# A list-scheduled hybrid decoder layer: inputs regrouped on the queues, weights in 4 KB runs, matmul costs taken from measured durations

## The chip, the cores and the metric

One Trainium2 chip, one core. The metric is the device time of one launch in microseconds (us). The kernel before takes 172.94 us (median of 3 runs, 172.69 to 173.69). PE is TensorE, DVE VectorE, ACT ScalarE, POOL GpSimd, SP SyncE, which issues most of the transfers.

## What is computed

One layer, T = 256 tokens, D = 1024, all in float32. The norm's reciprocal root is applied behind the projection, its gains ahead of it.

```
h = rmsnorm(x, pre_norm_g)
proj = einsum('btd,dc->btc', h, w_in)                 # 1024 x 4104
p_gdn, p_hgrn, p_moba, p_diff = split(proj)
y = concat([gdn_branch(p_gdn), hgrn2_branch(p_hgrn),
            moba_branch(p_moba), diff_branch(p_diff)])
x = x + rmsnorm(einsum('btc,cd->btd', y, w_out), post_norm_g)
```

Each branch has 4 heads of 64. The gated delta net (gdn) runs a short convolution over q, k and v, a gate g and, per chunk of 64 tokens, a triangular inverse; HGRN2 is a gated linear recurrence in chunks of 16; MoBA and the differential attention are causal softmax attentions with a distance penalty.

## The kernel before, in words

**The work.** The transposed x (1024 x 256, eight slices k of 128 rows) is scaled by the gains and split into a rounded high part `hT_hi` (ACT) and a remainder `hT_lo` (DVE). The weights come in pieces of two slices k and one of eight column blocks (512 columns, 520 for `gv`): 32 pieces of 512 KB, into six buffers `raw`. Each piece is split as well, `whi` on ACT and `wlo` on DVE (`split`, from line 423), into four buffers each, and each product is three matmuls, hi x hi, lo x hi and hi x lo, into `pj`. So no piece can reach PE before its transfer, one ACT instruction and one DVE instruction, and no buffer comes free before PE has used it. The first piece comes as two transfers (slices k = 0 and k = 1). `xs` is x once more, untransposed, for the norm and the residual sum.

**The first transfers** (lines 400 to 412, `piece` from 427). Five parts of the transposed x: the slice k = 0 on ACT's queue, the other four (k = 1; 2 and 3; 4 and 5; 6 and 7) on SP's queue between the weights. `pc` holds 35 columns of constants, the gains among them, and comes second on ACT's queue. A burst of bf16 matmuls on zeros (`wA<-g_nb`) runs on PE meanwhile.

**The order.** Every operation is recorded with a cost (`mm` 219, `act` 234, `vec` 240, `dma` 267) and `plan` (287) simulates the engines: of what is ready on an engine, the operation of the highest rank goes first. Rank is the longest path of costs to the end, plus a boost, plus `LEAD` of its part of the program (g is the delta net, h HGRN2, m and M MoBA, d and D the differential attention, o the output projection). `emit` (372) issues in that order, so nearly all instructions carry line 381 and table loads line 379. Three rules bend the order. Once PE has run an operation on part of its columns, others of that sort that are ready go ahead of full ones. An ACT function whose table set is not loaded waits while something else of a rank within `HOLD` is ready. A full matmul of 256 columns is charged 108.7 ns, a DVE subtraction of 1024 elements 1131 ns:

```
full = 1.667 if rhs.dtype == F else .417
... max(n * full, m * full, 53 if rhs.dtype == F else 107) + 2      # mm, PE
base = 66 if eng == "DVE" else 90                                   # vec
cost = base + (rate if eng == "DVE" else 2.2) * n + 61 * ...
```

On the chip nothing is simulated: each engine runs its list in order and waits on semaphores.

**Names.** `g_u`, `g_au`, `g_g`: the steps to the gate g, through ACT's exponential and logarithm. `g_ee`, `g_d`, `g_nb`, `g_y`, `g_ya`, `g_xa`: the triangular inverse on DVE, fifteen steps of one shuffle and two products; `g_xa` goes back to PE. `kf`, `lf`: keys and queries of the attentions; `wB<-kf,lf` their scores.

Of the kernel before, what the change touches and what calls it, by code (L numbers as in the profile page):

```python
# [21 lines left out]
F = mybir.dt.float32  # L22
# [3 lines left out]
AF = mybir.ActivationFunctionType  # L26
OP = mybir.AluOpType
# [62 lines left out]
class Op:  # L90
    __slots__ = ("eng", "fn", "args", "kw", "cost", "need", "preds", "succs", "rank", "left", "at", "order", "boost", "groups", "work", "part", "lat")


class Core:
# [72 lines left out]
    def record(self, eng, fn, cost, writes, reads, args, kw, need=None):  # L167
        op = Op()
        op.eng, op.fn, op.args, op.kw, op.cost, op.need = eng, fn, args, kw, cost, need
        op.preds, op.succs, op.boost, op.groups, op.work = set(), [], self.boost, (0, 1, 2, 3), 0.0  # L170
        op.part, op.lat = self.part, self.LAT[eng]
        me = len(self.ops)
        for w, aps in ((False, reads), (True, writes)):
            for ap in aps:
                name = ap.tensor.name
                if name in self.psum:

                    b = self.psum[name]
# [40 lines left out]
    def mm(self, out, lhsT, rhs, start=True, stop=True, **kw):  # L219
        n, m = self.size(rhs), lhsT.shape[1]  # L220
        full = 1.667 if rhs.dtype == F else .417
        self.record("PE", "matmul", max(n * full, m * full, 53 if rhs.dtype == F else 107) + 2, [out], [lhsT, rhs], (out,),
                    dict(lhsT=lhsT, rhs=rhs, start=start, stop=stop, **kw))
        p, m = self.rows(out)
        o = self.ops[-1]
        if 2 < m < 128:
            o.groups = tuple(range(p // 32, (p + m + 31) // 32))
        o.work = n * full * self.rows(rhs)[1] / 128

# [57 lines left out]
    def plan(self, noise=None):  # L287
# [21 lines left out]
        order, cur = [], 6  # L309
        cols, small, work = [0.0] * 4, False, {}  # L310
        while events:
# [5 lines left out]
            for e, q in ready.items():  # L317
# [76 lines left out]

def _build(c, x, xt, w_in, w_out, cst, pcol, prow, out, dbg):
    mm, tr, act = c.mm, c.tr, c.act
# [25 lines left out]

    BLOCKS = {"gkq": [(C_GQ, 512)], "gv": [(C_GV, 520)], "hqf": [(C_HQ, 512)], "hiz": [(C_HI, 512)],
              "mqk": [(C_MQ, 512)], "dqk": [(C_DQ, 512)], "mvz": [(C_MV, 512)], "dvz": [(C_DV, 512)]}
    RAW, HI, LO = {}, {}, {}

    def piece(key, k):

        if (key, k) not in HI:
            t = c.tmp("raw", [128, 2, 520], bufs=6)  # L430
            first = not HI
            (c0, w), = BLOCKS[key]
            part = w_in[k * 128:(k + 2) * 128, c0:c0 + w].rearrange("(k p) n -> p k n", p=128)
            lead = sum(1 for q in HI if q[0] != "o")
# [758 lines left out]
def _arrays(inputs):  # L1193
# [8 lines left out]
                                                      "diff_lq2", "diff_lk2", "post_norm_g")])[None]  # L1202
    return {"x": a["x"].reshape(T, D),
            "xt": np.ascontiguousarray(a["x"].reshape(T, 8, 128).transpose(2, 1, 0)).reshape(128, 8 * T),
            "w_in": a["w_in"][0], "w_out": a["w_out"][0], "cst": _shape_constants(),
            "pcol": np.ascontiguousarray(pcol), "prow": np.ascontiguousarray(prow)}

# [16 lines left out]
```

## Time and profile before

| | |
|---|---|
| median of 3 runs (lowest, highest) | 172.94 us (172.69, 173.69) |
| the profiled execution | 172.76 us |
| its span (first to last instruction) | 171.1 us |
| instructions | 3627 |
| transfers | 27.24 MB, 159 GB/s in the mean |
| ACT table loads | 17, 1283 ns each |
| `wlo` subtractions on DVE | 41, 1196 ns in the mean |

The profile is of one execution, so sums are made against its 172.76 us; 1.7 us of that lie outside the span. In the rows further below a line reads: start or busy time, engine, program line, operation, out<-in, shape, and in square brackets the idle time of the engine ahead of it with what ended that.

### The profile page before, as it was taken

Reading aid. Unit: us, or ns where it says so; the run is one execution under the profiler, and the core shown is the slowest. Engines: PE = TensorE matmul, PEld = TensorE weight load, DVE = VectorE, ACT = ScalarE, POOL = GpSimd, SP = SyncE. Lnnn points to the kernel's source line nnn. Section 1 sums busy time; section 2 is a strip of 40 time slices with the busy share of each in tenths; the row PEclk is TensorE's granted clock in tenths of the full one; section 3 lists DMA queues with packets and bytes.
Section 4 is the critical chain, followed back from the end, with each engine's and each line's share of the span. In section 5 each row is a group of like instructions: output and inputs, shape, how many; then the busy total and the mean of one; then the engine's idle time right before and its main releaser. Section 6 shows DMA issues by size and latency. Waiting matters only on the chain.

```text
span 171.1 us, 3627 instructions
## 1 busy us (share of the span) xinstructions
PE 161.9 (95%) x1358; PEld 141.9 (83%) x1358; DVE 132.2 (77%) x353; ACT 116.7 (68%) x219; POOL 15.7 (9%) x35
## 2 busy tenths in 40 slices
PE   7599999999999999999999999999999999999960
PEld 5399999999798999999799777776788878998850
DVE  0568559898988899999977968978798847559472
ACT  3375566799979864541299999989879925445440
POOL 8000000000000700000604106000000000000000
PEclk9999999999999999999999999999999999999998
DMA  4779997878872448619921998332702400000033
GB/s 137 259 269 322 368 352 264 336 254 236 181 266 87 91 130 206 159 15 256 265 52 40 216 339 254 81 128 63 245 0 98 151 0 0 4 0 0 0 123 123
DMA packets 14832, 27.24 MB, mean 159 GB/s; under 512 B 1504, under 2 KB 2784, under 8 KB 14816
## 3 DMA queue, kind: packets, MB, share of 16 engines
q1 hardware_dynamic: 13376, 25.30, 46.9%
q0 software_dynamic: 1152, 1.57, 4.2%
q8 instruction: 10, 0.16, 0.4%
q10 hardware_dynamic: 288, 0.15, 0.3%
q14 instruction: 6, 0.05, 0.1%
HBM read 24.14 MB, written 1.05 MB: 147 GB/s over the span
## 4 chain that ended last, share of the span: by engine, by line
PE 83%; DMA 8%; ACT 4%; DVE 1%; issue 1%; DVEq 0%; ACTq 0%
PE pj L381 58%; PE gB L381 8%; PE gA L381 7%; PE wB L381 6%; DMA raw<-in_w_in_dram 5%; PE wA L381 4%; DMA pc<-in_pcol_dram 3%; ACT whi L381 1%; ACT L379 1%; ACT qk4k L381 1%; DVE b4k L381 1%; DVE wlo L381 1%; ACT b4k L381 0%; DVEq L1220 0%; ACT hT_hi L381 0%
## 5 line engine op out<-in xcount | busy, mean ns | idle before, releaser
L381 DVE TENSOR_TENSOR wlo<-raw,whi 128x1024 fp32r<-128x1024 f32 (+2 forms) x41 | 48.0, 1196 | 10.5 <-ACT whi L381 7.8
L381 ACT ACTIVATE whi<-raw 128x1024 fp32r<-128x1024 f32 (+2 forms) x40 | 41.1, 1045 | 19.6 <-PE pj L381 9.5
L381 PE MATMUL pj<-hT_hi,whi 128*128 128x256 f32 x144 | 37.5, 293 | 2.1 <-ACT hT_hi L381 2.1
L381 PE MATMUL pj<-hT_lo,whi 128*128 128x256 f32 x144 | 37.3, 292 | 0.0
L381 PE MATMUL pj<-hT_hi,wlo 128*128 128x256 f32 x144 | 31.7, 292 | 0.0
L381 PEld LDWEIGHTS pj<-hT_hi,whi 128*128 128x128 f32 x144 | 27.4, 198 | 2.9 <-ACT hT_hi L381 2.6
L381 PEld LDWEIGHTS pj<-hT_lo,whi 128*128 128x128 f32 x144 | 27.1, 196 | 0.9 <-issue 0.7
L381 PE MATMUL pj<-whi,hT_lo 128*128 128x512 f32 (+2 forms) x80 | 26.6, 350 | 0.0
L381 PEld LDWEIGHTS pj<-hT_hi,wlo 128*128 128x128 f32 x144 | 23.6, 195 | 0.6 <-issue 0.3
L379 ACT ACT_TABLE_LOAD x17 | 21.8, 1283 | 2.0 <-PEq L1214 1.7
L381 PE MATMUL pj<-whi,hT_hi 128*128 128x512 f32 (+2 forms) x64 | 21.4, 350 | 0.0
L381 PE MATMUL pj<-wlo,hT_hi 128*128 128x512 f32 (+2 forms) x64 | 19.6, 347 | 0.0
L381 PEld LDWEIGHTS pj<-whi,hT_lo 128*128 128x128 f32 x80 | 15.0, 188 | 1.7
L381 PEld LDWEIGHTS pj<-whi,hT_hi 128*128 128x128 f32 x64 | 11.9, 188 | 1.4 <-issue 0.2
L381 PEld LDWEIGHTS pj<-wlo,hT_hi 128*128 128x128 f32 x64 | 10.9, 188 | 1.1
L381 ACT ACTIVATE prob<-prob,mx 128x128 f32<-128x128 f32 (+1 forms) x24 | 10.6, 445 | 0.5 <-DVE mx L381 0.5
L381 POOL DMA_DIRECT2D d_st<-d_ks x12 | 6.0, 509 | 51.2 <-ACT d_ks L381 51.2
L381 PE MATMUL pj<-whi,d_st 128*128 128x512 f32 (+1 forms) x32 | 9.6, 378 | 0.0
L381 POOL DMA_DIRECT2D d_st<-qk4k x12 | 5.9, 496 | 38.3 <-ACT qk4k L381 22.4
L381 DVE CUSTOM_DVE_ANT_0 prob<-wB,cs 128x128 f32<-128x128 f32 (+1 forms) x24 | 8.1, 351 | 1.7 <-PE wB L381 1.1
L381 PEld LDWEIGHTS pj<-whi,d_st 128*128 128x128 f32 x32 | 5.6, 188 | 1.1
L381 ACT ACTIVATE hT_hi<-prob,pc 128x256 fp32r<-128x256 f32 x8 | 3.7, 500 | 3.5 <-DMA pc<-in_pcol_dram 3.3
(266 smaller groups left out, 290.1 us busy)
## 6 DMA issues: line engine op xcount, KB each, us to landing
raw<-in_w_in_dram SPq DMA_DIRECT2D x27, 512.0 KB, 7.9
raw<-in_w_out_dram SPq DMA_DIRECT2D x8, 512.0 KB, 5.2
raw<-in_w_in_dram SPq DMA_DIRECT2D x4, 520.0 KB, 12.4
xs<-in_x_dram SPq DMA_DIRECT2D x2, 512.0 KB, 11.9
prob<-in_xt_dram SPq DMA_DIRECT2D x3, 256.0 KB, 7.7
d_st<-d_ks POOLq DMA_DIRECT2D x12, 64.0 KB, 2.1
d_st<-qk4k POOLq DMA_DIRECT2D x12, 64.0 KB, 4.3
raw<-in_w_in_dram SPq DMA_DIRECT2D x2, 256.0 KB, 4.1
```

The costliest lines, as they stand in the source:

```text
L379: nc.scalar.add_instruction(mybir.InstLoadActFuncSet(name=nc.get_next_instruction_name(), act_func_set_id=cur, ins=[], outs=[]))
L381: getattr(self.engines[o.eng], o.fn)(*o.args, **o.kw)
```

## The change

1. **Inputs.** The columns of constants and the transposed x are one array `pxt`. Its first 291 columns, the constants and the slice k = 0, come in one transfer into `px` (in the order `h_kd`, whose buffer it shares), and the four other parts of x follow it on ACT's queue. SP's queue starts with weights alone. The gains are read from `px`; `pc` is a copy made on DVE.
2. **Weights.** On the host, w_in is laid out piece by piece, so that a partition of a piece is one run of 4 KB in memory (4160 B for `gv`). In the buffer the two slices still stand 520 columns apart; only a piece of `gv` is one run there too.
3. **Scheduler.** A full matmul is charged `max(n * .446, 107) + 4.5` ns (256 columns: 118.7), each operation has a tile shape (`mode`), a change of shape is charged 95 ns and operations of the present shape are preferred; `HOLD` and `LEAD` get new values. The costs of DVE, ACT and the transfers stay.

```diff
-    HOLD = 1000
-    LEAD = {'h': -65, 'g': 9004, 'o': -15813, 'M': 4592, 'x': 3396, 'm': 1525, 'd': -18, 'D': 1459}
+    HOLD = 71859
+    SWITCH, KEEP, STAY = 95, 1e9, 10357
+    LEAD = {'h': 9467, 'g': 7491, 'o': -78342, 'M': -634, 'x': 25587, 'm': 2702, 'd': 2886, 'D': 6239}
...
-        self.record("PE", "matmul", max(n * full, m * full, 53 if rhs.dtype == F else 107) + 2, [out], [lhsT, rhs], (out,),
+        cost = max(n * full, m * full) + 2 if rhs.dtype == F else max(n * .446, 107) + 4.5
+        self.record("PE", "matmul", cost, [out], [lhsT, rhs], (out,),
...
+        k = self.rows(rhs)[1]
+        o.mode = (32 if k <= 32 else 64 if k <= 64 else 128 if k > 96 else 96, 32 if m <= 32 else 64 if m <= 64 else 128)
+        o.work = n * full * k / 128
...
-                if e == "PE" and small and len(o.groups) == 4:
-
-                    more = [x for x in q if len(ops[x[1]].groups) < 4]
+                if e == "PE" and mode != o.mode:
+
+                    more = [x for x in q if ops[x[1]].mode == mode and -x[0] > o.rank - (self.KEEP if mode != (128, 128) else self.STAY)]
...
-                    was, small = small, len(o.groups) < 4
-                    o.at = max([t] + [cols[g] + 53 * was * (1 if small else .5) for g in o.groups])
+                    if o.mode != mode:
+                        o.at = max(t, max(cols) + self.SWITCH)
+                        mode = o.mode
+                    else:
+                        o.at = max([t] + [cols[g] for g in o.groups])
...
-    XPARTS = [(0, 1), (1, 2), (2, 4), (4, 6), (6, 8)]
...
+    c.boost = turn(0)
+    c.dma(px[:, 0:P_END + T], pxt[:, 0:P_END + T], "ACT")
+    XPARTS = [(1, 2), (2, 4), (4, 6), (6, 8)]
...
-        c.dma(xr[a // 2][:, a % 2:a % 2 + b - a], xt[:, a * T:b * T].rearrange("p (k t) -> p k t", t=T), "ACT" if a == 0 else "SP")
-    c.boost = turn(0) - 0.1 * BOOST
-    c.dma(pc, pcol, "ACT")
+        c.dma(xr[a // 2][:, a % 2:a % 2 + b - a],
+              pxt[:, P_END + a * T:P_END + b * T].rearrange("p (k t) -> p k t", t=T), "ACT")
...
-            part = w_in[k * 128:(k + 2) * 128, c0:c0 + w].rearrange("(k p) n -> p k n", p=128)
+            w, o = BLOCKS[key], BLOCK_AT[key] + k * 128 * BLOCKS[key]
+            part = bass.AP(tensor=w_in.tensor, offset=w_in.offset + o, ap=[[2 * w, 128], [w, 2], [1, w]])
```

**How the order moves.** Buffer numbers are shifted by one between the two programs (`whi_93` before is `whi_94` in the change), and line 381 becomes 392.

ACT at the start of the program, first before, then in the change (`prob_67` to `prob_71` and `h_kd` hold x):

```order
L381 DMA prob_67<-in_xt_dram 128x256
L381 DMA pc<-in_pcol_dram 128x35
L379 ACT_TABLE_LOAD
L381 ACTIVATE hT_hi<-prob_67,pc 128x256
L381 ACTIVATE whi_93<-raw_92 128x512
L381 ACTIVATE hT_hi<-prob_67,pc 128x256
L381 ACTIVATE whi_96<-raw_95 128x2x512
L381 ACTIVATE hT_hi<-prob_68,pc 128x256 x2
L381 ACTIVATE whi_99<-raw_98 128x2x512
```

```order
L392 DMA h_kd<-in_pxt_dram 128x291
L392 DMA prob_68<-in_pxt_dram 128x256
L392 DMA prob_69<-in_pxt_dram 128x512
L392 DMA prob_70<-in_pxt_dram 128x512
L392 DMA prob_71<-in_pxt_dram 128x512
L390 ACT_TABLE_LOAD
L392 ACTIVATE hT_hi<-h_kd 128x256
L392 ACTIVATE hT_hi<-prob_68,h_kd 128x256
L392 ACTIVATE whi_94<-raw_93 128x512
L392 ACTIVATE hT_hi<-prob_69,h_kd 128x256 x2
L392 ACTIVATE hT_hi<-prob_70,h_kd 128x256
L392 ACTIVATE whi_97<-raw_96 128x2x512
```

The table load now stands behind five transfers, the scaling of slice k = 4 (`hT_hi<-prob_70`) stands ahead of the `whi` of slices 2 and 3, and the scaling of both halves of `prob_69` comes ahead of it too.

PE where the attention scores `wB<-kf,lf` (64 rows) stand among the projection's matmuls, before and in the change:

```order
L381 MATMUL pj_106<-hT_hi,whi_102 128x256
L381 MATMUL wB_147<-kf,lf 128x128
L381 MATMUL pj_106<-hT_lo,whi_102 128x256
L381 MATMUL pj_106<-hT_hi,wlo_103 128x256
L381 MATMUL pj_106<-hT_hi,whi_102 128x256
L381 MATMUL pj_106<-hT_lo,whi_102 128x256
L381 MATMUL pj_106<-hT_hi,wlo_103 128x256
L381 MATMUL wB_147<-kf,lf 128x128
L381 MATMUL pj_106<-hT_hi,whi_102 128x256
L381 MATMUL pj_106<-hT_lo,whi_102 128x256
```

```order
L392 MATMUL pj_91<-whi_103,hT_lo 128x256
L392 MATMUL pj_92<-hT_hi,whi_103 128x256
L392 MATMUL pj_92<-hT_lo,whi_103 128x256
L392 MATMUL wA_78<-ident,prob_68 128x128
L392 MATMUL gA_83<-g_xa,g_ee 64x64 x16
L392 MATMUL wB_148<-kf,lf 128x128 x2
L392 MATMUL wA_78<-ident,prob_68 128x128
L392 MATMUL pj_92<-hT_hi,whi_103 128x256
L392 MATMUL pj_92<-hT_lo,whi_103 128x256
L392 MATMUL pj_91<-wlo_95,hT_hi 128x256
```

The score matmuls, each alone before, now go in pairs, later, and some of them right behind another small shape. Counted over both programs, PE leaves the full shape 29 times before and 23 times in the change. The matmul `gA<-g_xa` stands 67 matmuls earlier than before.

DVE at the start of the triangular inverse, before and in the change:

```order
L381 SCALAR_TENSOR_TENSOR g_d_128<-g_ee,cs,g_d_128 128x128
L381 TENSOR_TENSOR g_kdec<-gA_82,g_kd 64x2x128
L381 SCALAR_TENSOR_TENSOR g_d_128<-g_ee,cs,g_d_128 128x128
L381 TENSOR_TENSOR wlo_100<-raw_92,whi_99 128x2x512
L381 STREAM_SHUFFLE g_nb_76<-g_d_128 128x128
L381 TENSOR_TENSOR wlo_103<-raw_95,whi_102 128x2x512
L381 TENSOR_TENSOR g_nb_76<-g_nb_76,g_y_129 128x8x15
L381 STREAM_SHUFFLE g_nb_130<-g_d_128 128x128
L381 TENSOR_TENSOR g_y_129<-g_y_129,g_nb_76 128x8x15
L381 STREAM_SHUFFLE g_nb_131<-g_d_128 128x128
L381 TENSOR_TENSOR g_nb_130<-g_nb_130,g_y_129 128x8x14
```

```order
L392 SCALAR_TENSOR_TENSOR g_d_129<-g_ee,cs,g_d_129 128x128
L392 TENSOR_TENSOR g_kdec<-gA_83,g_kd 64x2x128
L392 STREAM_SHUFFLE g_nb_77<-g_d_129 128x128
L392 STREAM_SHUFFLE g_nb_131<-g_d_129 128x128
L392 TENSOR_TENSOR g_nb_77<-g_nb_77,g_y_130 128x8x15
L392 STREAM_SHUFFLE g_nb_132<-g_d_129 128x128
L392 TENSOR_TENSOR wlo_95<-raw_108,whi_94 128x2x512
L392 TENSOR_TENSOR g_y_130<-g_y_130,g_nb_77 128x8x15
L392 TENSOR_TENSOR g_vb<-gB_115,g_beta 64x2x128
L392 TENSOR_TENSOR wlo_98<-raw_109,whi_97 128x2x512
L392 TENSOR_TENSOR g_nb_131<-g_nb_131,g_y_130 128x8x14
L392 TENSOR_TENSOR wlo_101<-raw_93,whi_100 128x2x512
```

Four `wlo` of 1024 elements now stand within the first steps of the inverse; before, seven stand within all of it. On ACT the list of the change has 9 table loads, that of before 17.

## Rows read from the trace of the kernel before

**Rows 1.** The page, parts 1 and 4: busy time by engine, and the chain by engine.

```profile
PE 161.9 (95%) x1358; PEld 141.9 (83%) x1358; DVE 132.2 (77%) x353; ACT 116.7 (68%) x219; POOL 15.7 (9%) x35
...
PE 83%; DMA 8%; ACT 4%; DVE 1%; issue 1%; DVEq 0%; ACTq 0%
```

**Rows 2.** The chain of waits, in order of time: start us, us, what.

```profile
1.23 4.96 DMA pc<-in_pcol_dram
6.85 15.73 PE pj L381 x108
...
72.62 9.35 PE pj L381 x79
81.97 1.06 PE wB L381 x4
```

**Rows 3.** Busy time of the engines from 60 to 88 us, x instructions: PE, PEld, DVE, ACT, POOL.

```profile
60.00:88.00 28.00, 28.00 (x232) 26.53 (x233) 27.17 (x107) 13.48 (x22) 2.92 (x6) 1.00 0.66 165
```

**Rows 4.** Timeline of PE: start us, us, engine line op out<-in xcount.

```profile
51.55 0.28 PE L381 MATMUL pj<-hT_hi,whi 128*128 128x256 f32 x1
51.76 0.48 PE L381 MATMUL wB<-kf,lf 64*128 64x128 f32 x2
52.18 0.38 PE L381 MATMUL pj<-hT_lo,whi 128*128 128x256 f32 x1
52.40 0.28 PE L381 MATMUL pj<-hT_hi,wlo 128*128 128x256 f32 x1
```

**Rows 5.** Timeline of ACT and PE in the head; idle before in square brackets.

```profile
0.80 0.40 ACTq L381 DMA_DIRECT2D prob<-in_xt_dram  x1
...
6.28 0.51 ACT L381 ACTIVATE hT_hi<-prob,pc 128x256 fp32r<-128x256 f32 x1 [3.27 <-DMA pc<-in_pcol_dram]
...
6.85 0.79 PE L381 MATMUL pj<-hT_hi,whi 128*128 128x256 f32 x2 [2.10 <-ACT hT_hi L381]
...
8.56 1.06 ACT L381 ACTIVATE whi<-raw 128x1024 fp32r<-128x1024 f32 x1 [0.85 <-DMA raw<-in_w_in_dram]
...
11.54 0.41 PE L381 MATMUL pj<-hT_hi,wlo 128*128 128x256 f32 x1
...
12.55 0.28 PE L381 MATMUL pj<-hT_hi,wlo 128*128 128x256 f32 x1
```

**Rows 6.** DMA issues in flight at 1.2 and at 2.2 us: KB each, us to landing.

```profile
prob<-in_xt_dram ACTq DMA_DIRECT2D x1, 128.0 KB, 3.5
pc<-in_pcol_dram ACTq DMA_DIRECT2D x1, 17.5 KB, 5.0
...
raw<-in_w_in_dram SPq DMA_DIRECT2D x1, 512.0 KB, 6.4
```

**Rows 7.** The same columns in the first 12 us; clock, DMA share and GB/s last.

```profile
0.00:4.00 4.00, 2.85 (x14) 2.04 (x15) 0.23 (x3) 1.28 (x1) 3.37 (x11) 1.00 0.42 133
4.00:8.00 4.00, 1.90 (x9) 1.25 (x7) 1.67 (x5) 1.43 (x3) 0.56 (x1) 1.00 0.68 240
8.00:12.00 4.00, 4.00 (x20) 4.00 (x20) 2.92 (x5) 2.40 (x4) 0.00 (x0) 1.00 0.83 311
```

**Rows 8.** Timeline of ACT, DVE and PE around the gate g_g.

```profile
42.89 1.28 ACT L379 ACT_TABLE_LOAD   x1
...
44.13 0.16 DVE L381 TENSOR_TENSOR g_g<-g_u,nea 128x8 f32<-128x8 f32 x1
...
44.50 0.51 PE L381 MATMUL gA<-g_g,cs 128*128 128x8 f32 x4
```

**Rows 9.** Timeline of DVE and PE around the triangular solve.

```profile
59.61 0.42 DVE L381 TENSOR_TENSOR g_ee<-gA,g_ee 128x256 f32<-128x256 f32 x1 [0.46 <-PE gB L381]
...
74.15 4.62 DVE L381 TENSOR_TENSOR wlo<-raw,whi 128x1024 fp32r<-128x1024 f32 x4
...
86.08 0.70 DVE L381 STREAM_TRANSPOSE g_xa<-g_ya 128x512 f32<-128x512 f32 x1
...
87.59 1.15 PE L381 MATMUL gA<-g_xa,g_ee 64*64 64x64 f32 x32
```

More of the change, by code (lines that the diff above doesn't have):

```diff
@@ L39 @@
 C_DQ, C_DK, C_DV, C_DZ = 3080, 3336, 3592, 3848
+W_BLOCKS = (("gkq", C_GQ, 512), ("gv", C_GV, 520), ("hqf", C_HQ, 512), ("hiz", C_HI, 512),
+            ("mqk", C_MQ, 512), ("dqk", C_DQ, 512), ("mvz", C_MV, 512), ("dvz", C_DV, 512))
 K_TRI, K_AFT, K_BLK, K_BM, K_I16 = 0, 128, 256, 288, 292
@@ L90 @@
 class Op:
-    __slots__ = ("eng", "fn", "args", "kw", "cost", "need", "preds", "succs", "rank", "left", "at", "order", "boost", "groups", "work", "part", "lat")
+    __slots__ = ("eng", "fn", "args", "kw", "cost", "need", "preds", "succs", "rank", "left", "at", "order", "boost", "groups", "work", "part", "lat", "mode")
 class Core:
@@ L170, in record @@
         op.preds, op.succs, op.boost, op.groups, op.work = set(), [], self.boost, (0, 1, 2, 3), 0.0
-        op.part, op.lat = self.part, self.LAT[eng]
+        op.part, op.lat, op.mode = self.part, self.LAT[eng], (128, 128)
         me = len(self.ops)
@@ L227, in mm @@
             o.groups = tuple(range(p // 32, (p + m + 31) // 32))
-        o.work = n * full * self.rows(rhs)[1] / 128
+        k = self.rows(rhs)[1]
+        o.mode = (32 if k <= 32 else 64 if k <= 64 else 128 if k > 96 else 96, 32 if m <= 32 else 64 if m <= 64 else 128)
+        o.work = n * full * k / 128
     def tr(self, out, in_, ident):
@@ L309, in plan @@
         order, cur = [], 6
-        cols, small, work = [0.0] * 4, False, {}
+        cols, mode, work = [0.0] * 4, (128, 128), {}
         while events:
@@ L359, in plan @@
                         cols[g] = end
-                    free[e] = end if len(o.groups) == 4 else o.at + 53 * slow
+                    free[e] = end if len(o.groups) == 4 else o.at + 7 * slow
                 heapq.heappush(events, (free[e], 1, -1))
@@ L381, in emit, with build @@
             getattr(self.engines[o.eng], o.fn)(*o.args, **o.kw)
-def build(tc, x, xt, w_in, w_out, cst, pcol, prow, out, dbg=None):
+def build(tc, x, pxt, w_in, w_out, cst, prow, out, dbg=None):
     with ExitStack() as ctx:
-        _build(Core(ctx, tc), x, xt, w_in, w_out, cst, pcol, prow, out, dbg)
+        _build(Core(ctx, tc), x, pxt, w_in, w_out, cst, prow, out, dbg)
 def bc(ap, n):
@@ L392, in bc, with _build @@
     return ap.unsqueeze(len(s)).to_broadcast(s + [n])
-def _build(c, x, xt, w_in, w_out, cst, pcol, prow, out, dbg):
+def _build(c, x, pxt, w_in, w_out, cst, prow, out, dbg):
     mm, tr, act = c.mm, c.tr, c.act
@@ L401, in _build @@
     xs = c.tile("xs", [128, 2, D])
+    px = c.tile("px", [128, 512], tag="h_kd")
     pc = c.tile("pc", [128, P_END])
@@ L420, in _build @@
           base=0, channel_multiplier=-1)
-    BLOCKS = {"gkq": [(C_GQ, 512)], "gv": [(C_GV, 520)], "hqf": [(C_HQ, 512)], "hiz": [(C_HI, 512)],
-              "mqk": [(C_MQ, 512)], "dqk": [(C_DQ, 512)], "mvz": [(C_MV, 512)], "dvz": [(C_DV, 512)]}
+    BLOCKS, BLOCK_AT, o = {}, {}, 0
+    for key, c0, w in W_BLOCKS:
+        BLOCKS[key], BLOCK_AT[key] = w, o
+        o += w * D
     RAW, HI, LO = {}, {}, {}
@@ L431, in piece @@
             first = not HI
-            (c0, w), = BLOCKS[key]
-            part = w_in[k * 128:(k + 2) * 128, c0:c0 + w].rearrange("(k p) n -> p k n", p=128)
+            w, o = BLOCKS[key], BLOCK_AT[key] + k * 128 * BLOCKS[key]
+            part = bass.AP(tensor=w_in.tensor, offset=w_in.offset + o, ap=[[2 * w, 128], [w, 2], [1, w]])
             lead = sum(1 for q in HI if q[0] != "o")
@@ L482, in _build @@
         c.boost = BOOST + 500.0
-        g = pc[:, P_PRE + k:P_PRE + k + 1]
-        act(hh_t[:, k], xr[k // 2][:, k % 2], AF.Copy, scale=g)
-        c.stt(hl_t[:, k], xr[k // 2][:, k % 2], g, hh_t[:, k].bitcast(F), OP.mult, OP.subtract)
+        g = px[:, P_PRE + k:P_PRE + k + 1]
+        xk = xr[k // 2][:, k % 2] if k else px[:, P_END:P_END + T]
+        act(hh_t[:, k], xk, AF.Copy, scale=g)
+        c.stt(hl_t[:, k], xk, g, hh_t[:, k].bitcast(F), OP.mult, OP.subtract)
     c.boost = 0.0
+    c.copy(pc, px[:, 0:P_END])
+    c.ts(pc[:, P_GAIN + 2:P_GAIN + 3], pc[:, P_GAIN + 2:P_GAIN + 3], 1.0 - lam_init, None, OP.mult)
     rs = c.tile("rs", [128, 2])
@@ L559, in _build @@
     GAIN = {"gdn": P_GAIN, "hgrn": P_GAIN + 1, "diff": P_GAIN + 2}
-    c.ts(pc[:, P_GAIN + 2:P_GAIN + 3], pc[:, P_GAIN + 2:P_GAIN + 3], 1.0 - lam_init, None, OP.mult)
     def finish_y(name, y, bank):
@@ L1202, in _arrays @@
                                                       "diff_lq2", "diff_lk2", "post_norm_g")])[None]
[L1203 to L1206, printed above, removed]
+    xt = a["x"].reshape(T, 8, 128).transpose(2, 1, 0).reshape(128, 8 * T)
+    blocks = [a["w_in"][0][:, c0:c0 + w].reshape(4, 2, 128, w).transpose(0, 2, 1, 3).reshape(-1) for _, c0, w in W_BLOCKS]
+    return {"x": a["x"].reshape(T, D), "pxt": np.ascontiguousarray(np.concatenate([pcol, xt], axis=1)),
+            "w_in": np.concatenate(blocks)[None], "w_out": a["w_out"][0], "cst": _shape_constants(),
+            "prow": np.ascontiguousarray(prow)}
 def kernel(**inputs):
```

## The prediction, written before the change was run

> **What bounds the kernel now.** I read the page first. PE is busy for 95% of the span and holds 83% of the chain that ended last [rows 1]; DVE and ACT have more room in the mean. Then the chain in order of time: it starts with 4.96 us of the transfer of `pc`, and from 6.85 us on it is PE nearly all the way [rows 2]. So two things set the time: when PE starts, and how long its stream is. The mean hides a third. From 60 to 88 us DVE is busy for 27.17 of 28 us [rows 3]: there PE and DVE end together, and whoever hastens PE alone meets DVE.
>
> The timeline of PE gives its prices. 79 projection matmuls in a row start 0.118 us apart (9.35 / 79) [rows 2]. A change of tile shape shows at the scores: the matmul ahead of the pair starts 0.21 us before it (51.55, 51.76) and the one behind it 0.22 before the next (52.18, 52.40) [rows 4], some 0.19 over twice 0.118. The pair itself takes 0.42 for two rows of 128 columns; four rows of 256 columns take 1.06 [rows 2]. With p for 256 columns and e for the edges, 4p + e = 1.06 and p + e = 0.42, so e is 0.21. A round trip out of the full shape and back costs some 0.40 here.
>
> **The change, part by part.** A difference of 0.5%, 0.86 us, is about what a measurement of this kernel can tell from no change. The profiled execution, 172.76 us, lies 0.18 under the median of 172.94; the sum stands on 172.76.
>
> *Shapes.* The new list leaves the full shape 23 times, the old one 29; the matmuls are the same. Six round trips at 0.40 are 2.4 us; if the merged pieces had only the outer edges of 0.19, it would be 1.1. Most are scores like those of rows 4, some the delta net's small squares, so I take -1.9 (-2.4 to -1.1).
>
> *Start.* PE's first real matmul (6.85) waits for `hT_hi` (6.28), which waits for the gains in `pc` [rows 5], not for x: x was issued at 0.80 [rows 5] and took 3.5 us, `pc` took 5.0 [rows 6]. Now both come with the first transfer, which should land at about 4.4. Five issues at 0.43 (0.80 to 1.23) put the table load [1.28 us, rows 8] at 2.95, done at 4.23: in time, though only just. `hT_hi` then starts at 4.6, the first matmul at 5.2, which is 1.65 earlier.
>
> *Is it kept?* 15 matmuls now stand ahead of the first that needs the weights of slices 2 and 3; before it was 21. At 20 in 4 us [rows 7] PE has them done at 8.2. That `whi` needs its 512 KB, and ACT's list puts the scaling of slice 4 ahead of it, which came in the fourth transfer on ACT's own queue. A queue does not go ahead of the other: 17.5 KB of `pc` took 5.0 us beside the weights [rows 6]. If they move side by side, 1.0 MB of weights and 0.8 MB of x have to be in. At 133, 240 and 311 GB/s in the three stretches [rows 7], 0.53 MB are in at 4 us, 1.49 at 8 and 1.8 at 9.0; with 1.06 for the `whi` [rows 5] it is ready at about 10.1. Before, PE had done (10.1 - 6.85) / 0.20 = 16 matmuls by then, so 15 is no gain: I take 0. Below: if the 512 KB land 6.4 us after their issue, as before [rows 6], now half a microsecond earlier, about -0.9, and with no wait at all -1.65. Above: PE's matmuls last 0.41 at 11.54 and 0.28 at 12.55 [rows 5], the lower and the higher of its two clock levels (1.2 and 2.4 GHz), though the granted clock reads 1.00 throughout [rows 7]. The rise came 5.7 us after the first real matmul, without a pause. A pause of 1.8 us in the head may put it off; three and a half microseconds more at 0.20 a matmul in place of 0.118 would cost 1.4.
>
> Here a rule of the Trainium skill bears on the change. The share of the DMA engines is 0.42 and 0.68 in the first two stretches [rows 7], which reads as if there were room for x beside the weights; by that the weights are not delayed, and the sum is 0.9 less, 172.9. The skill's page "Trainium Kernel Development and Optimization", section Key Constraints, says that transfers issued from SP, ACT and POOL run on the same 16 DMA engines and interleave, and that a second issuing engine only saves issue time; by that the sum stays at 173.8. The late `pc` of rows 6 agrees with the page.
>
> *Weights in runs of 4 KB.* The pieces still go to two runs of 2 KB per partition in the buffer, only `gv` to one. PE waits for no weights between 60 and 88 us, at 100% busy [rows 3], so a faster transfer is hidden: 0. In the head it would be worth the part "below" of the start.
>
> *Table loads.* Eight fewer at 1.28 [rows 8], 10.3 us of ACT. ACT is 4% of the chain [rows 1], so this is hidden too, and if its cover goes it is a gain only: 0, though it takes a share of waits that I count next.
>
> *New waits.* PE's matmuls were charged 108.7 ns and take 118: the old list held PE to be 8% faster than it is, so DVE and ACT had that much to spare on the chip. Now PE is charged right, DVE still too little: 1131 ns for a `wlo` that takes 1.155 us back to back (4.62 / 4) [rows 9], and more in small steps. So its results should come late where the list puts them just in time.
>
> First place, the triangular inverse. Before, DVE worked from `g_ee` at 59.61 to `g_xa`, which ended at 86.78; PE took it up at 87.59 [rows 9], 0.8 later: no wait. That are 27.2 us with seven `wlo`. Now four stand between; 27.2 - 3 x 1.155 is 23.7, less about 1.2 for softmax and gate work that stands elsewhere: 22.5. From the last `gB<-qk4k`, which releases DVE, to `gA<-g_xa` PE's new list has 161 matmuls at 0.118, nine transposes of about the same and one pair of scores: 19.0 + 1.1 + 0.8 = 20.9. With about 0.3 for the two handovers PE comes 1.9 too early: +1.9 (0 if the inverse holds less work than I think, 3 if DVE starts late as well). Behind `gA<-g_xa` on PE stand all the rest, and whatever ACT and DVE do with it.
>
> Second place, the gate. Before, `g_g` ended at 44.29, and PE took it up at 44.50 [rows 8]: just in time. Now, behind the PE matmul that frees a `whi` buffer, ACT runs that `whi`, a table load, `g_au`, another `whi` and `g_au`, then DVE `g_u` and `g_g`: 1.06 + 1.28 + 1.06 + four small ones of 0.2 or less = 4.1, with three handovers of about 0.2 some 4.6. PE has 37 matmuls until it asks, 4.4. I take +0.5 (0, and up to 1.4 where DVE is inside a `wlo` just then).
>
> The rest, small waits at the inverse's later rounds and the attention: +0.5 (0 to 1.5). The output projection and the tail have the same list: 0.
>
> The sum: 172.76 - 1.9 + 0 + 0 + 0 + 1.9 + 0.5 + 0.5 = 173.76, about **173.8**. The extremes of the terms give 172.76 - 2.4 - 1.65 = 168.7 and 172.76 - 1.1 + 1.4 + 3 + 1.4 + 1.5 = 179.0; not all fall together.
>
> **Rivals.** *A, not slower: DVE is in time.* The place is `gA<-g_xa`, and the point from which it decides is an inverse of under 20.6 us between its release and `g_xa`. Its price, 1.9 us, then goes, and the gate's and the rest's waits with it, for they come from the same undercharge: 172.76 - 1.9 = 170.9, and 169.3 if the start is kept as well. For it: DVE's first steps can overlap more, and fewer table loads free ACT. Against it: DVE's 97% in rows 3.
>
> *B, the head is worse.* The five transfers of x on ACT's queue hold back the first weights, PE pauses after 15 matmuls and the clock rises late: +1.4 in the place of 0, 175.2, and 176.3 with a late inverse of 3. For it: one transfer more stands ahead of what PE needs third. Against it: rows 7, where the engines are not full.
>
> *C, it cancels.* The start is kept by half (-0.9) and the waits are as summed: 172.9. The layout and the fewer table loads do nothing, and the new list wins at shapes what it loses in waits.
>
> **How the numbers follow.** The forecast's own case, the start given back and waits of 2 to 4 us (172.9 to 174.9), gets 0.42, of which 0.30 is over +0.5% and 0.12 within. A gets 0.32, nearly all of it under -0.5%. B gets 0.14, slower. C gets 0.12, within but for 0.02. So faster 0.31, same 0.23, slower 0.46. The range runs from 170.0, which takes in A without its lowest part, to 176.5, the upper end of B: outside of it lie some 2 in 10. The forecast's own range is 172.9 to 174.9.
>
> **What would show it.** In the profile of the changed kernel: the first `pj` matmul at about 5.2, and an idle time of PE of 1 to 2.5 us between 8 and 10.5 ended by the `whi` of slices 2 and 3; an idle time of PE ahead of `gA<-g_xa` of 1 to 3 us, ended by DVE; one ahead of `gA<-g_g` of up to 1.4; about 23 pairs of edges at 0.19; nine table loads. The forecast is wrong if `g_xa` is done before PE asks, if PE runs through from 5.2 us on, or if the weights of the head land clearly earlier than 9 us.

## The result and the profile after

The change takes 174.73 us (median of 20 runs, 172.97 to 175.66), the kernel before 173.28 (20 runs, 172.68 to 173.74). The runs of the change fall into two groups, eight of 172.97 to 173.76 and twelve of 174.25 to 175.66 with the profiled one (175.41, span 173.7) among them, and the ratio to before leaves out the two longest: 1.0064, with a 95% interval of 1.0036 to 1.0093. The change is slower by 0.6%, a little over what can be told from no change; 173.8 was forecast, the way was right, and the range held it.

The page of the change, parts 1 and 4, as [rows 1] of before: PE is busy 1.1 us less, but its share of the chain falls from 83% to 74%, and DVE's rises from 1% to 12%.

```profile
PE 160.8 (93%) x1358; PEld 140.1 (81%) x1358; DVE 132.9 (77%) x354; ACT 106.8 (61%) x211; POOL 15.7 (9%) x35
...
PE 74%; DVE 12%; DMA 7%; ACT 2%; issue 1%; ACTq 1%; DVEq 0%
```

The head, as [rows 7]: busy time of PE, PEld, DVE, ACT and POOL, then granted clock, DMA share and GB/s. PE has more done by 8 us, half of a stretch idle from 8 to 12, and a granted clock of 0.50 and 0.68 in the two stretches where the matmuls are 0.21 us apart (in the second up to 14.4 us); the transfers run at 335 and 406 GB/s where they had 240 and 311.

```profile
0.00:4.00 4.00, 2.85 (x14) 1.99 (x15) 0.23 (x3) 0.78 (x1) 3.37 (x11) 1.00 0.50 149
4.00:8.00 4.00, 2.96 (x16) 2.00 (x15) 2.67 (x7) 2.38 (x5) 0.56 (x1) 0.97 1.00 335
8.00:12.00 4.00, 2.11 (x10) 1.82 (x9) 2.82 (x5) 3.42 (x7) 0.00 (x0) 0.50 1.05 406
12.00:16.00 4.00, 4.00 (x25) 4.00 (x25) 3.27 (x5) 2.90 (x6) 0.00 (x0) 0.68 1.02 415
```

The timeline of ACT and PE in the head, as [rows 5]. The first matmul starts at 5.33. The 15 matmuls are done at 8.7, and PE is idle for 1.89 us until the `whi` of slices 2 and 3 at 10.57. That `whi` stood behind the scaling of slice 4, which waited for x until 9.06. From 5.86 on the matmuls last about 0.28 (the higher of PE's two clock levels), from 7.84 on 0.41 (the lower), before and after the pause, and 0.30 or less again only from 14.57 on.

```profile
4.52 0.51 ACT L392 ACTIVATE hT_hi<-h_kd 128x256 fp32r<-128x256 f32 x1
...
5.33 0.35 PE L392 MATMUL pj<-hT_hi,whi 128*128 128x256 f32 x1 [0.82 <-DVE whi L392]
...
7.58 0.28 PE L392 MATMUL pj<-hT_lo,whi 128*128 128x256 f32 x1
...
8.27 0.41 PE L392 MATMUL pj<-hT_hi,wlo 128*128 128x256 f32 x1
9.06 0.51 ACT L392 ACTIVATE hT_hi<-prob,h_kd 128x256 fp32r<-128x256 f32 x1 [0.47 <-DMA prob<-in_pxt_dram]
...
9.47 1.04 ACT L392 ACTIVATE whi<-raw 128x1024 fp32r<-128x1024 f32 x1
...
10.57 0.58 PE L392 MATMUL pj<-hT_hi,whi 128*128 128x256 f32 x1 [1.89 <-ACT whi L392]
...
14.14 0.41 PE L392 MATMUL pj<-hT_lo,whi 128*128 128x256 f32 x1
...
14.57 0.30 PE L392 MATMUL pj<-hT_lo,whi 128*128 128x256 f32 x1
```

The waits of PE in the whole program (us in total, times, longest). Before, beside the start of the zeros, there were two:

```profile
PE pj L381 <- ACT hT_hi L381: 2.1, 1, 2.1
...
PE gB L381 <- ACT b4k L381: 0.2, 1, 0.2
```

Now the first row and 0.2 of the `wlo` row are the head's, the others stand in the stream, and DVE ends most of them.

```profile
PE pj L392 <- ACT whi L392: 1.9, 1, 1.9
PE pj L392 <- DVE g_nb L392: 1.4, 1, 1.4
...
PE pj L392 <- DVE wlo L392: 1.0, 2, 0.7
...
PE pj L392 <- DVE gz_moba L392: 0.5, 1, 0.5
PE gA L392 <- ACT g_eb L392: 0.4, 1, 0.4
```

Of PE's 1343 matmul records I took the time from each start to the next. Behind the 100th, the 428 of small shapes (64 or 32 rows or columns) take 23.4 us before and 21.1 now, and the gaps of over 0.12 us above the usual spacing add up to 0.3 us before and 4.0 now. So the stream from the 100th to the last is 143.6 us before and 145.1 now, and the 100th starts at 21.4 and 22.6: of the loss in the profiled execution 1.5 us are in the stream and 1.1 in the head. All such sums of a trace are those of one execution, not of the median.

### The profile page after: what moved, and what is told of

Read it like the earlier page. It is cut to its first block, busy times and chain, and to the rows that moved or that the text cites. A ratio compares the mean times of both kernels' runs of the same rounds, so it can differ in the third digit from the quotient of the medians.

```text
span 173.7 us, 3605 instructions
## 1 busy us (share of the span) xinstructions
PE 160.8 (93%) x1358; PEld 140.1 (81%) x1358; DVE 132.9 (77%) x354; ACT 106.8 (61%) x211; POOL 15.7 (9%) x35
## 4 chain that ended last, share of the span: by engine, by line
PE 74%; DVE 12%; DMA 7%; ACT 2%; issue 1%; ACTq 1%; DVEq 0%
PE pj L392 49%; PE gA L392 7%; PE gB L392 7%; PE wB L392 6%; PE wA L392 6%; DVE wlo L392 5%; DMA prob<-in_pxt_dram 4%; DMA raw<-in_w_in_dram 3%; DVE g_nb L392 2%; ACT whi L392 1%; DVE g_vb L392 1%; ACTq L392 1%; DVE g_y L392 1%; DVE b4k L392 1%; DVE lf L392 1%
## 5 line engine op out<-in xcount | busy, mean ns | idle before, releaser
L392 DVE TENSOR_TENSOR wlo<-raw,whi 128x1024 fp32r<-128x1024 f32 (+2 forms) x41 | 48.1, 1197 | 11.1 <-ACT whi L392 6.4
L392 PE MATMUL pj<-hT_hi,whi 128*128 128x256 f32 x144 | 38.8, 293 | 4.1 <-ACT whi L392 1.9
L392 PE MATMUL pj<-hT_lo,whi 128*128 128x256 f32 x144 | 38.1, 290 | 0.0
L392 PEld LDWEIGHTS pj<-hT_hi,whi 128*128 128x128 f32 x144 | 28.1, 196 | 6.0 <-ACT whi L392 3.8
L392 PE MATMUL pj<-hT_hi,wlo 128*128 128x256 f32 x144 | 28.9, 292 | 0.2 <-DVE wlo L392 0.2
L392 PEld LDWEIGHTS pj<-hT_lo,whi 128*128 128x128 f32 x144 | 28.1, 197 | 0.1
L392 PEld LDWEIGHTS pj<-hT_hi,wlo 128*128 128x128 f32 x144 | 22.2, 194 | 0.9 <-DVE wlo L392 0.6
L392 PE MATMUL pj<-wlo,hT_hi 128*128 128x512 f32 (+2 forms) x64 | 21.3, 348 | 0.7 <-DVE wlo L392 0.7
L392 PE MATMUL pj<-whi,hT_hi 128*128 128x512 f32 (+2 forms) x64 | 21.4, 342 | 0.5 <-DVE gz_moba L392 0.5
L392 PEld LDWEIGHTS pj<-wlo,hT_hi 128*128 128x128 f32 x64 | 11.6, 188 | 2.3 <-DVE wlo L392 1.1
L392 ACT ACTIVATE prob<-prob,mx 128x128 f32<-128x128 f32 (+1 forms) x24 | 10.7, 448 | 3.4 <-DVE mx L392 3.3
L392 PE MATMUL pj<-whi,d_st 128*128 128x512 f32 (+1 forms) x32 | 10.1, 390 | 0.0
L392 POOL DMA_DIRECT2D d_st<-qk4k x12 | 5.9, 492 | 13.5 <-PE wB L392 11.8
L392 ACT ACTIVATE t2k<-pj 128x512 f32<-128x512 f32 (+1 forms) x4 | 2.2, 544 | 5.3 <-PE pj L392 5.3
```

Source lines behind the costliest of these rows:

```text
L392: getattr(self.engines[o.eng], o.fn)(*o.args, **o.kw)
```

## The experiments

Theory of the forecast: the scheduler loses in the stream, because PE is charged right and DVE too little; in the head x and the weights get in each other's way. Rivals: only the head loses; HOLD and LEAD, not the charge, make the waits; the layout does nothing. Each time is a median; the kernel before, run beside them, took 173.0 to 173.4, and the last column is the ratio to it.

| kernel | us | ratio to before, 95% interval |
|---|---|---|
| the change | 174.73 | 1.0036 to 1.0093 |
| inputs and layout, old scheduler (`old_sched`) | 170.96 | 0.9858 to 0.9934 |
| scheduler alone (`sched_only`) | 176.62 | 1.0149 to 1.0212 |
| the change, old layout (`old_layout`) | 177.25 | 1.0201 to 1.0282 |
| the change, x on SP's queue (`x_on_sp`) | 177.03 | 1.0186 to 1.0243 |
| the change, old charge (`old_charge`) | 171.07 | 0.9854 to 0.9918 |
| the change, old HOLD and LEAD (`old_lead`) | 181.95 | 1.0456 to 1.0556 |
| the change, DVE charged more (`dve_charged`) | 173.63 | 0.9984 to 1.0039 |
| the change, pause filled (`fill`) | 173.69 | 1.0009 to 1.0052 |
| the same, `d_ks` early (`dks_early`) | 173.58 | 0.9999 to 1.0042 |
| old charge, head filled (`charge_fill`) | 170.90 | 0.9842 to 0.9906 |
| old charge, x on SP's queue, split order (`x_on_sp2`) | 172.49 | 0.9926 to 0.9974 |
| old charge, x on both queues (`x_split`) | 170.62 | 0.9835 to 0.9864 |

### Which part loses

The change with the class of the scheduler taken from the kernel before (its charge, HOLD, LEAD, no `mode`):

```diff
-    HOLD = 71859
-    SWITCH, KEEP, STAY = 95, 1e9, 10357
+    HOLD = 1000
...
-                if e == "PE" and mode != o.mode:
+                if e == "PE" and small and len(o.groups) == 4:
```

> Parts 1 and 2 of the change (inputs, layout) with the scheduler of before (its costs, HOLD, LEAD, no tile shapes). Forecast's reading: shapes lose 1.9 us again, the new waits of some 3.3 us behind DVE go, the head stays as in the change: about 172 to 173.5, with no wait of PE over 0.5 us between 20 and 160 us. Rival, the head carries the loss: 174 to 175.5.

It took 170.96 us, less than either kernel. PE has the pause in the head (1.6 us) and no gap of over 0.12 us between full matmuls behind its 100th. And the kernel before with only the new scheduler, the same diff the other way round:

> The kernel before with part 3 alone (scheduler). Forecast's reading: -1.9 for shapes, +3.3 for waits behind DVE (one of over 1 us near the triangular inverse), the head as before: 174 to 175. Rival, the head carries the loss and the scheduler alone gains: 170.5 to 172.

176.62, more than forecast: gaps of 1.0 us at 74 and of 1.5 in two at 108 and 109, and smaller ones at 23, 26 and 68. Held against before as run beside them (173.40), inputs and layout win 2.4 us and the scheduler loses 3.2; that makes a loss of 0.8, and the two together lose 1.45, so the parts nearly add up.

The layout, with every list left as it is (`w_in` is handed over in its rows again):

```diff
...
-            part = bass.AP(tensor=w_in.tensor, offset=w_in.offset + o, ap=[[2 * w, 128], [w, 2], [1, w]])
+            part = w_in[k * 128:(k + 2) * 128, C0[key]:C0[key] + w].rearrange("(k p) n -> p k n", p=128)
...
```

> The change with the weights laid out as before (2 KB runs in memory); the order of every engine is that of the change. If the layout is worth nothing, as forecast, the time stays within 0.5 us of the change (174.2 to 175.2) and a 512 KB piece still takes 5.9 us to landing. If the layout is what made the transfers faster, the median landing goes back to about 7.9 us; then the weights of slices 2 and 3 land a microsecond later than 9.2 and the time is 175 to 176.5, unless PE's pause in the head is set by x alone, in which case the landing grows and the time stays.

The forecast of no effect fell: 177.25, 2.5 us more than the change in the median and 1.3 more between the profiled executions (176.69 to 175.41), all of it in the head: the 100th matmul starts 1.5 us later. The median landing of all pieces does not show it (5.8 us to 5.9). The head does; the two stretches from 4 to 12 us with the old layout, to be held against those of the change above, and the `whi` of slices 2 and 3 with PE behind its pause:

```profile
4.00:8.00 4.00, 2.67 (x11) 1.93 (x9) 2.79 (x7) 2.82 (x4) 0.56 (x1) 1.00 0.78 246
8.00:12.00 4.00, 2.04 (x10) 1.64 (x9) 1.69 (x5) 2.58 (x5) 0.00 (x0) 1.00 0.90 314
```

```profile
10.75 1.04 ACT L393 ACTIVATE whi<-raw 128x1024 fp32r<-128x1024 f32 x1
...
11.84 0.38 PE L393 MATMUL pj<-hT_hi,whi 128*128 128x256 f32 x1 [1.96 <-ACT whi L393]
```

246 and 314 GB/s in the place of 335 and 406, the first matmul at 5.86 in the place of 5.33, and the `whi` of slices 2 and 3 1.3 us later (10.75 for 9.47). The weights under it landed only 0.4 later; it is x of slice 4, scaled ahead of it on ACT, that landed 1.3 later (10.3 for 9.0). The old layout changes the length of a run and its distance to the next (rows of 16416 B) together, so which of the two counts was not separated.

### What makes the waits

The charge alone:

```diff
-        cost = max(n * full, m * full) + 2 if rhs.dtype == F else max(n * .446, 107) + 4.5
+        cost = max(n * full, m * full) + 2 if rhs.dtype == F else max(n * .417, 107) + 2
```

> The change with one formula of before: a full matmul of 256 columns is charged 108.7 ns again; tile shapes, HOLD and LEAD of the change stay. Its list has 21 matmuls ahead of the weights of slices 2 and 3, as the run with the whole old scheduler had, so the head should be that one's (100th matmul at about 20.0 us, 2.6 earlier than in the change). If the charge makes the waits behind DVE, they go as well: no wait of PE over 0.5 us between 20 and 160 us and about 169.5 to 171. If HOLD and LEAD make them, they stay, some 3 us: 171.5 to 173.

171.07, with tile shapes, HOLD and LEAD of the change left in. PE has 16 matmuls ahead of its pause, not 21. Of the 4.7 us between the profiled executions 2.2 are in the head, up to the 100th matmul (20.4 for 22.6 us), and 2.5 behind it. Its waits in the same view as above, all that are listed but the start of the zeros; the upper two are in the head:

```profile
PE pj L392 <- ACT whi L392: 0.9, 1, 0.9
PE pj L392 <- DVE whi L392: 0.7, 1, 0.7
PE gB L392 <- DVE ath L392: 0.2, 1, 0.2
PE gA L392 <- DVE y L392: 0.2, 1, 0.2
```

HOLD and LEAD alone put back:

```diff
-    HOLD = 71859
+    HOLD = 1000
...
-    LEAD = {'h': 9467, 'g': 7491, 'o': -78342, 'M': -634, 'x': 25587, 'm': 2702, 'd': 2886, 'D': 6239}
+    LEAD = {'h': -65, 'g': 9004, 'o': -15813, 'M': 4592, 'x': 3396, 'm': 1525, 'd': -18, 'D': 1459}
```

> The change with HOLD and LEAD of before; the new charge and the tile shapes stay. Its head is that of the change, 15 matmuls ahead of the pause. If HOLD and LEAD make the waits behind DVE, they go and the time is 171.5 to 173; if the charge makes them, waits of 2 to 4 us stay (perhaps at other places): 174 to 176.

A miss for both readings: 181.95, with waits of 2.7 us behind DVE `y` at 159 us and 1.4 at `gA<-g_xa`:

```profile
84.63 1.20 PE L392 MATMUL gA<-g_xa,g_ee 64*64 64x64 f32 x32 [1.39 <-DVE m_sum L392]
...
159.01 1.19 PE L392 MATMUL gA<-whi,y_gdn 128*128 128x256 f32 x4 [2.68 <-DVE y L392]
```

So these values do not make the waits; with the new charge the old ones make worse ones. Then the other side of the balance, DVE charged nearer to what it takes:

```diff
-        base = 66 if eng == "DVE" else 90
+        base = 100 if eng == "DVE" else 90
```

> The change with every DVE operation charged 34 ns more (a subtraction of 1024 elements 1165 ns). If the undercharge of DVE makes the new waits, the planner now sees them and places work ahead of them: the wait of 1.4 us behind DVE in the triangular inverse and those around 107 us fall to under 1 us together, 172 to 173.5 with the change's head. If the planner has nothing to put there, or the waits come of HOLD and LEAD, they stay: 174 to 175.5.

173.63: the waits at 72 and 107 us are gone, two smaller ones (0.5 and 0.7) came at 129 and 153. Again 15 matmuls stand ahead of the pause, but they and the first ones behind it are 0.12 apart, and the 100th starts 0.45 earlier than in the change. A charge that flatters PE and one that is nearer right for both engines each remove the waits at 72 and 107 us, which agrees with a lost balance; it is one other list, so it does not prove it. And the waits are not all: the new list gives back half of the gain in small shapes (22.2 us, 21.1 in the change, 23.4 before), and it stays 2.6 us behind `old_charge`.

Whether DVE as a whole is late in the triangular inverse, or one operation stands wrongly. The change, `d_ks` and PE around the wait:

```profile
71.11 0.69 DVE L392 TENSOR_TENSOR d_ks<-pj,rrow 128x512 f32<-128x512 f32 x1
...
78.28 0.71 DVE L392 STREAM_TRANSPOSE g_xa<-g_ya 128x512 f32<-128x512 f32 x1
...
70.22 0.28 PE L392 MATMUL pj<-hT_hi,whi 128*128 128x256 f32 x1
71.94 0.35 PE L392 MATMUL pj<-hT_hi,whi 128*128 128x256 f32 x1 [1.44 <-DVE g_nb L392]
...
79.07 1.14 PE L392 MATMUL gA<-g_xa,g_ee 64*64 64x64 f32 x31
```

PE stops at 70.5 for an accumulator that `d_ks` still has to read; the row names `g_nb`, the DVE operation that ended last. `g_xa` is done at 78.99, just as PE asks. In the next run `d_ks` stands ahead of the inverse's four `wlo`:

```diff
...
+        order.remove(dks)
+        order.insert(order.index(wlo), dks)
```

> The run that filled PE's pause, with one DVE operation more ahead: d_ks, which frees PE's accumulator in the middle of the triangular inverse, goes in front of the inverse's four wlo. If DVE as a whole is late there (the forecast's reading), the wait of 1.4 us ahead of the pj matmul goes and comes back at another place that waits for DVE within 10 us, gA<-g_xa above all; the time stays at 173.3 to 174. If only the place of d_ks was wrong, the wait is gone for good: 172.0 to 172.7.

Held against the run it was built on (`fill`, below), matmul by matmul, PE is 1.8 us ahead behind that place, 1.15 ahead at 77 us and 0.04 behind at 79. The two waits that took its place (ahead of the second, ACT had waited 2.8 us for DVE's `mx`):

```profile
72.37 0.38 PE L402 MATMUL pj<-hT_hi,whi 128*128 128x256 f32 x1 [0.39 <-DVE qk4k L402]
...
77.61 0.33 PE L402 MATMUL wA<-ident,prob 128*128 128x128 f32 x1 [1.10 <-ACT prob L402]
```

The wait moved, the time stayed (173.58 to 173.69). DVE as a whole is late there.

The wait at 107 us is a ring through DVE, in the chain of the change: a `wlo` frees a buffer only at 98.8, the transfer into it takes 5.93 us, then ACT and DVE split it.

```profile
97.58 1.23 DVE wlo L392
98.82 5.93 DMA raw<-in_w_in_dram
104.84 1.07 ACT whi L392
105.93 1.23 DVE wlo L392
```

### The head

PE's pause filled with 12 bf16 matmuls on zeros:

```diff
...
+        order = order[:b] + [pe[0]] * 12 + order[b:]
```

> The change with 12 more bf16 matmuls on zeros on PE behind its 15th projection matmul, where PE pauses for 2.1 us. If the pause is what keeps PE at its lower clock level until 14.4 us, the matmuls behind it run at 0.12 apart, and the time is 172.5 to 173.5. If the level falls for another reason (it fell at 7.8 us, ahead of the pause), 12 matmuls at 0.21 last 2.5 us, PE starts 0.4 later and the time is 174.7 to 175.5.

173.69, and a spread of 1.2 us (172.94 to 174.15) in the place of 2.7. Its stretches from 8 to 16 us:

```profile
8.00:12.00 4.00, 4.00 (x24) 3.23 (x23) 2.34 (x4) 3.10 (x6) 0.00 (x0) 0.61 1.00 393
12.00:16.00 4.00, 4.00 (x36) 4.00 (x36) 3.74 (x6) 2.90 (x5) 0.00 (x0) 1.00 1.02 415
```

The matmuls come to a spacing of 0.12 at 11.1 us, 3.3 earlier than in the change, and from 15 us to 97 PE runs 1.23 us ahead of the change, matmul by matmul; at the end it is 1.65. With the old charge, where the pause is shorter, filling it and the gap ahead of the first matmul brings nothing:

```diff
...
+        order = order[:a] + [pe[0]] * 3 + order[a:b] + [pe[0]] * 8 + order[b:]
```

> The change with the old charge of a matmul (171.07 us), with 3 bf16 matmuls on zeros ahead of PE's first real one and 8 in its pause. If PE's rest in the head keeps its matmuls at 0.21 (13 of them were, up to 8.8 us), those go to 0.12 and nothing else changes: 169.5 to 170.6. If what is won in the head is given back later, as it was by two fifths in the run that filled the pause, 170.5 to 171. If the level does not follow: 171 to 171.8.

170.90 to 171.07: its matmuls were 0.12 apart from 7.5 us on, and it waited then until 10.41 for the same `whi`. The landing sets the end of the head there, not the clock.

Where x should travel. First all of it back on SP's queue, the lists otherwise left:

```diff
...
+        for i, after in zip(xd, (sp[1], sp[2], sp[3], sp[4])):
+            self.ops[i].eng = "SP"
+            order.insert(order.index(after) + 1, i)
```

> The change with the four later parts of x back on SP's queue, each behind the weights' transfer that it stood behind before; nothing else moves. If x on a queue of its own takes bandwidth from the weights of slices 2 and 3, these land before 8.5 us in place of 9.2 and PE's pause of 1.9 us in the head falls below 1; x of slices 4 and 5 lands later, though, and its scaling stands ahead of that whi on ACT, so the pause may move there. If the pause shrinks the matmuls stay at 0.28 and the time is 172.5 to 173.5. If only the sum of bytes counts, pause and time stay: 174.2 to 175.2.

A miss: 177.03, and a pause of 3.22 us. x of slices 4 and 5 now came behind 1.9 MB on one queue. It was issued at 4.08 in the place of 2.21 and landed at 10.7 in the place of 9.0, and ACT scales it ahead of the `whi`. In the change (chain of waits) and here (issue, ACT and PE):

```profile
2.21 6.83 DMA prob<-in_pxt_dram
```

```profile
4.08 0.60 SPq L398 DMA_DIRECT2D prob<-in_pxt_dram  x1
...
10.73 0.51 ACT L398 ACTIVATE hT_hi<-prob,h_kd 128x256 fp32r<-128x256 f32 x1 [2.19 <-DMA prob<-in_pxt_dram]
...
12.24 0.39 PE L398 MATMUL pj<-hT_hi,whi 128*128 128x256 f32 x1 [3.22 <-ACT whi L398]
```

Then, on the old charge, with the splits ahead of the scaling:

```diff
...
+        for eng, a, b in (("ACT", "whi", "hT_hi"), ("DVE", "wlo", "hT_lo")):
...
+                    order.insert(order.index(to), i)
```

> The change with the old charge, the four later parts of x on SP's queue between the weights as in the kernel before, and on ACT and DVE the splits of slices 2 to 7 ahead of the scaling of the same slices, as before too; so the merged first transfer and the layout stay of the head. If x on a queue of its own holds the weights back, those of slices 2 and 3 land before 8 us and PE's pause of 1.3 us goes: 169.5 to 170.7. If only the order on ACT counted (x of slices 4 and 5 ahead of the weights of 2 and 3), the same. If the sum of bytes counts, the pause moves to the next weights: 171 to 172.

172.49, 1.4 more than with x on ACT's queue. The weights of slices 2 and 3 were in by 7.5 us, as the first reading had it, and PE then waited for x: three gaps of 1.0, 0.5 and 1.1 us from start to start, for `hT_hi` and `hT_lo`, and matmuls at 0.21 from 11.8 to 15.1. Last, still on the old charge, only the two transfers of x that are needed late go to SP's queue (`hi` and `lo` are the scalings, `w` and `v` the splits):

```diff
...
+        for i, j, behind in ((xd[0], sp[3], 1), (xd[1], sp[4], 1), (w[1], hi[4], 0), (w[2], hi[4], 0), (w[3], hi[6], 0), (v[2], lo[4], 0)):
+            order.remove(i)
+            order.insert(order.index(j) + behind, i)
```

> The change with the old charge of a matmul (171.07 us); x of slices 4 to 7 leaves ACT's queue for SP's, behind the weights of slices 4 and 5 and of 6 and 7, and on ACT and DVE those slices are scaled behind the weights of slices 2 and 3. So 1.5 MB in place of 1.9 have to land before PE's 17th matmul. If the sum of bytes ahead of them is what holds back the weights of slices 2 and 3, their whi is ready by about 8.5 us in place of 10.1, PE's pause of 1.3 us goes, everything behind shifts with it, and the time is 169.3 to 170.3. If the pause only moves to the next weights or to x of slices 4 and 5: 170.6 to 172.

170.62 (five runs, 170.52 to 170.74), the lowest time and the narrowest spread, though not clear of `old_charge`, whose interval overlaps. ACT in its head: the `whi` of slices 2 and 3 starts at 8.16, 0.87 us earlier than in `old_charge` and 1.3 earlier than in the change, and PE meets it without a pause of note.

```profile
8.16 1.04 ACT L404 ACTIVATE whi<-raw 128x1024 fp32r<-128x1024 f32 x1
9.36 1.07 ACT L404 ACTIVATE whi<-raw 128x1024 fp32r<-128x1024 f32 x1 [0.17 <-DMA raw<-in_w_in_dram]
```

The order on ACT moved as well, so the `whi` alone does not tell what helped. The landing of its weights does: from issue to landing they took 7.5 us in the change, 7.1 in `old_charge` and 6.3 here.

```profile
raw<-in_w_in_dram SPq DMA_DIRECT2D x1, 512.0 KB, 7.5
```

```profile
raw<-in_w_in_dram SPq DMA_DIRECT2D x1, 512.0 KB, 7.1
```

```profile
raw<-in_w_in_dram SPq DMA_DIRECT2D x1, 512.0 KB, 6.3
```

By profile 0.74 us are won on `old_charge` at 12 us, 0.37 are left behind the next weights and 0.10 at the end. That is the second reading, the pause only moves on: the gain is in the spread more than in the best run.

## Why the prediction was right, and where it was not

- **Shapes, -1.9.** Right: the small shapes take 2.3 us less from start to start.
- **Start, 5.2 us.** Right: 5.33, and the table load was in time (`hT_hi` at 4.52).
- **"Is it kept?", 0.** The pause came where it was put, 1.89 us for 1.8, and the matmuls came back to 0.12 late, which stood in the upper bound and in rival B: at the 100th matmul the profiled execution is 1.1 us behind before. So its head is rival B's, and its 175.41 is near B's 175.2. The landing, forecast at 9.0, came at 9.0 for x and 9.2 for the weights, by two errors that offset each other. What failed in the working is "1.0 MB of weights and 0.8 MB of x have to be in": at 149 and 335 GB/s 1.94 MB had moved by 8 us, and x and weights were not in. The engines moved faster, but they also moved transfers that are needed later. `x_split`, which puts two of these behind the weights, has the weights in 0.8 us sooner after their issue than `old_charge`.
- **Weights in 4 KB runs, 0.** Wrong, and the largest miss: 2.5 us in the median and 1.3 between the profiled executions, by `old_layout`. The step was "PE waits for no weights, so a faster transfer is hidden"; in the head PE's start and its pause both ended on landings. The prediction had a price for that, the part "below" of the start, and did not put it into the sum. "Two runs of 2 KB in the buffer" was no reason either: the rate rose by a third.
- **The triangular inverse, +1.9.** Right in cause and about in size (a wait of 1.4, a gap of 1.6), wrong in place: not `gA<-g_xa` but the accumulator that `d_ks` frees, seven microseconds ahead. `g_xa` was done at 78.99 and PE took it up at 79.07 without a wait, which the prediction had named as a sign that it is wrong. `dks_early` shows why the price still came: with the first wait gone PE loses the same time ahead of that very matmul, to a softmax result that waits for DVE.
- **The gate, +0.5.** Nearly nothing: no wait at `gA<-g_g`, which starts at 41.16, 0.11 behind the matmul ahead of it.
- **The rest, +0.5.** Too small: 1.5 at 107 to 109 us, and 0.5 at 53.9 behind `g_eb`.
- **Table loads, 0.** There were nine, as counted; no run separates what they are worth.
- **Rule against row.** The reading of the row, room for x beside the weights, failed: the share of the engines was 1.00 from 4 us on, and the weights of slices 2 and 3 took 7.5 us to landing where they had taken 6.4 [rows 6]. The other reading, that they are delayed, held in kind, but at 335 GB/s and not at 240. The page of the Trainium skill named there ("Trainium Kernel Development and Optimization", Key Constraints) says that transfers of several issuing engines interleave on the same 16 DMA engines and that a second issuing engine only saves issue time. `x_on_sp` agrees: on SP's queue x of slices 4 and 5 was issued 1.87 us later and landed 1.7 later. It also shows that issue time is not always small: the kernel took 2.3 us more (177.03 to 174.73; 1.4 between the profiled executions, nearly all of it in the pause), because a `whi` stood behind that x on ACT.

That the total came out near the forecast is in part luck. The sum was +1.0, the profiled execution is +2.65: -2.3 for shapes, +3.7 for waits, +1.1 for the head and 0.15 that I did not place. The median lies 0.7 below that execution, and no term stood for this. In the head a gain that I had set at nothing, the layout, and a loss that I had only in the bounds offset each other; without that gain the time is 177.25, outside the range.

## What to carry to other kernels

A list scheduler with one wrong charge may be balanced by another; correcting the charge of one engine takes the slack from the rest, so look at every place where a result is just in time. Correcting DVE's charge too took the two largest waits away and was still no faster than the kernel before (`dve_charged`), while the wrong charge was (`old_charge`): a list is judged by its time, not by its charges. A layout that PE does not feel in the stream can still matter where it waits for landings, here the head: look at GB/s by stretch, not at the median landing. And if an engine is late as a whole, moving its one late operation moves the wait.

## What the runs showed of the hardware

- With the pieces in 4 KB runs of memory the queues of the head moved 335 and 406 GB/s where 2 KB runs out of rows of 16416 B gave 246 and 314 (4 to 8 and 8 to 12 us), though all but the `gv` pieces go to the buffer 2 KB at a time in both.
- PE's matmuls of 256 columns were 0.12 or 0.21 us apart in the head and 0.12 later. A pause does not decide it alone: `old_sched` ran at 0.12 ahead of its pause of 1.6 us and behind it; the change went to 0.21 at 7.8 us, ahead of its pause, and back to 0.12 at 14.4, and with the pause filled at 11.1. What decides was not settled.
- The granted clock read 1.00 in the stretches up to 12 us of before [rows 7] with matmuls of 0.41, and 0.50 and 0.68 in those of the change; so the durations were the surer sign in before.
- A shift won in the head can last: 1.23 us won at 15 us by filling the pause were 1.23 at 97 us, at the same matmul, with most of the program's matmuls between. It need not: of the 0.37 us that `x_split` was ahead of `old_charge` at 40 us, 0.11 were left at 100.
